# First weights in column pieces over two queues, and masked copies and taps at other steps, in a gated-merge decoder layer

## The chip, the cores and the metric

The kernel runs on one core of a Trainium2 chip (trn2). The metric is device time in microseconds (us): the median over runs of the whole program. A difference of a few tenths of a per cent is what such a comparison of this kernel can tell.

## The reference

One layer of a decoder works on 256 tokens of 2048 features. All weights are f32.

```python
h = rmsnorm(x, norm_mix_g)
c, b, xa, za, q, f, iv, og, ga, gb = split(h @ w_in)   # 8 x 1024 and 2 x 2048 columns
ya = b * causal_dwconv3(c * xa, conv_w) * silu(za)     # branch A, a convolution with three taps
lb = clip(...)                                         # lower bound, from lb_param
log_f = logaddexp(log(lb), log1p(-lb) + log_sigmoid(f))
kk = (1 - lb) * sigmoid(-f)
o = hgrn2_chunked(silu(q), kk, iv, log_f)              # branch B: gated linear recurrence, 8 heads of 128
yb = per_head_rmsnorm(o) * hg_norm_g * silu(og)
m = sigmoid(ga) * (ya @ w_a_out) + sigmoid(gb) * (yb @ w_b_out)
x = x + m @ w_o
x = x + sigmoid(rmsnorm(x, ple_norm_g) @ w_ple_gate) * (p @ w_ple_proj)
return rmsnorm(x, final_norm_g)
```

Here p is a second input of 256 tokens by 256 features. The recurrence over the tokens of a head is o_t = q_t . state, with state = exp(log_f) * state + k v.

## The kernel before

**Products.** Every large product runs over a stream of weight chunks. A chunk has 256 rows (two k-tiles of 128) by 512 columns, that is 128 partitions by 1024 f32, 512 KB. TensorE multiplies in an f32 form of reduced width (fp32r), so both operands are split into a high and a low part: `split(pos)` copies a chunk with ScalarE to `whi` (L124) and subtracts with VectorE to `wlo` (L125); `put` and `put_p` do the same for the activations. Three products (high x high, high x low, low x high) for two token tiles and two k-tiles make 12 matmuls of 512 columns for each chunk (`product`, L945).

**Order.** A list of groups, and in it of chunks, is the stream: four groups for p @ w_ple_proj with one chunk each (tile name `pT`, stored in the buffers `yaTh` and `yaTl`), then w_in, w_a, w_b, w_o and w_ple_gate. The main loop goes over the positions of the stream. Ahead of the matmuls of a position it splits the chunks up to `LEAD` = 3 positions further, and behind them it advances the open epilogues by one step each. Epilogues are generators: a `yield` ends a step, so the place of a piece of work among the matmuls is set by the number of `yield`s ahead of it. A scheduler then orders each engine's instructions, and each engine runs its own in order. The high and low parts of chunks have four buffers each.

**The start.** SyncE issues nearly all DMAs, in order. The first are p (both k-tiles in one transfer, L154), the second half of chunk 0 and chunk 1 (L111), the parameters `prm_t` (L158), then chunk 2, a quarter of x, chunk 3, and so on alternately (L815 to L817). ScalarE's queue issues the first half of chunk 0 (L111). Ten matmuls on a zeroed tile warm up TensorE (`WARM`, L820 to L825). For the first chunk `put_p(i)` and a split of half i are taken in turn, and the first k-tile's products are taken by kind, high x high first, low parts of the weights last:

```python
for n in ((0,), (2,), (1,)) if pos == 0 and i == 0 else ((0, 1, 2),):
    for t in range(NT):
        product(psum[t], state[opname], k, t, hi[:, s], lo[:, s], k == 0, k == 2 * nch - 1, n)
```

**The recurrence.** `hgrn(j)`, j = 0 and 1, handles four heads each. It works on 128 tokens with a hierarchy of levels (`LEVELS`): for each level a pair of operands `X` is made, multiplied on TensorE in many small matmuls (`products`, L389), and the parts that belong to the level are kept by masked copies (`keep`, COPY_PREDICATED). The four small levels are collected in a tile `both`; two masked copies then bring `both` into the two blocks of `a` (L511). `kT` and `qT` are scaled in place (L509, L510) for the last pairs, which TensorE multiplies at L530.

**The taps.** `ep_xa(j)` multiplies c and xa, transposes the product through DRAM (`turned`) and applies the three taps of the convolution for four feature tiles: one on ScalarE (L608) and two on VectorE (L617), in steps.

Of the kernel before, what the change touches and what calls it, by code (L numbers as in the profile page):

```python
# [9 lines left out]
F32 = mybir.dt.float32  # L10
# [5 lines left out]
P = 128  # L16
T = 256
NT = T // P
# [5 lines left out]
CW = 512  # L24
PLE = 256
EPS = 1e-6
WARM = 10
LB_FLOOR = 1e-30
LB_MAX = 1.0 - 1e-6
SCAN = 64  # L30
# [14 lines left out]
def hybrid_kernel(ctx, tc, xT, x, pT, prm, gfin, masks, w_in, w_a, w_b, w_o, w_pg, w_pp, out):  # L45
    nc = tc.nc
# [31 lines left out]
    def t4(tag="t4", bufs=None):  # L78
        bufs = bufs or {"tmp1": 8, "tmp2": 5, "tmp3": 5}[state["tmp"]]
        return pools[state["tmp"]].tile([P, 1024], F32, tag=tag, bufs=bufs, name=nm(tag))  # L80
# [13 lines left out]
    def load(pos):  # L94
        w, g, c = stream[pos]
        if pos // 2 not in loaded:
            raw = wp.tile([P, 2, 2 * CW], F32, tag="raw", bufs=3, name=nm("raw"))
            loaded[pos // 2] = raw
            if FIRST <= pos < FIRST + 4:
                for i in range(2):  # L100
                    nc.sync.dma_start(out=raw[:, i, :], in_=w[g, :, c + i, :])
            elif pos >= FIRST:
                nc.sync.dma_start(out=raw, in_=w[g, :, c : c + 2, :])
        return loaded[pos // 2]

    def load_first(pos, queues):

        w, g, c = stream[pos]
        n = 2 * CW // len(queues)
        for i, eng in enumerate(queues):  # L110
            eng.dma_start(out=load(pos)[:, pos % 2, i * n : (i + 1) * n], in_=w[g, :, c, i * n : (i + 1) * n])  # L111

    def split(pos, halves=(0, 1)):
        w, g, c = stream[pos]
        src = load(pos)[:, pos % 2, :]

        pool, n = (pools["late"], 6) if (pos - state.get("late", len(steps))) % 10 < 6 and "late" in state else (wp, 4)
        if pos not in parts:
            parts[pos] = tuple(
                pool.tile([P, 2 * CW], F32R, tag=tag, bufs=n, name=nm(tag)) for tag in ("whi", "wlo")  # L120
            )
        hi, lo = parts[pos]
        s = slice(halves[0] * CW, (halves[-1] + 1) * CW)
        a = nc.scalar.activation(out=hi[:, s], in_=src[:, s], func=AF.Copy)  # L124
        v = nc.vector.tensor_tensor(  # L125
            out=lo[:, s], in0=src[:, s], in1=hi[:, s].bitcast(F32), op=ALU.subtract
        )
        state["splits"] = (a.ins, v.ins)
# [22 lines left out]
    FIRST = 6  # L151

    praw = t4()[:, : 2 * T]
    nc.sync.dma_start(out=praw.rearrange("p (k t) -> p k t", k=2), in_=pT)  # L154
    load_first(0, (nc.scalar, nc.sync))
    load_first(1, (nc.sync,))
    prm_t = const.tile([P, PRM_N], F32, name="prm_t")
    nc.sync.dma_start(out=prm_t, in_=prm)  # L158

    if PAD_CONST:  # L160
        nc.gpsimd.memset(const.tile([P, PAD_CONST], F32, name="pad"), 0.0)
# [189 lines left out]
    def hgrn(j):  # L351
# [122 lines left out]
        for i in range(4):  # L474
            keep(both, 2 + i, heads(bk), 32 * i)
        Xs.append(level(LEVELS[1]))
        yield
        yield
        yield

        e = t4()
# [25 lines left out]
        for blk in range(2):  # L507
            kk, qq = k2[:, :, blk, :, 1 - blk, 0], q2[:, :, blk, :, 1 - blk, 0]
            nc.vector.tensor_tensor(out=kk, in0=kk, in1=rv[:, :, blk], op=ALU.mult)  # L509
            nc.gpsimd.tensor_tensor(out=qq, in0=qq, in1=fv[:, :, blk], op=ALU.mult)  # L510
            nc.vector.copy_predicated(  # L511
                out=a[:, blk],
                mask=mask_t[:, len(LEVELS) + blk : len(LEVELS) + blk + 1, :].to_broadcast([P, 4, P]), data=both,
            )
        yield
        yield
        bo = bank("s")
# [75 lines left out]
    def ep_xa(j, psum):  # L593
        cx = t4()
        plain_times(psum, state["c", j], cx)
        cxT = yield from turned(cx, 4)
        cv = t4("cv", 1)
        for h in range(2):
            for i in range(2):
                n = h * 2 + i  # L600
                k = j * 4 + n
                d, s = cv[:, n * T : (n + 1) * T], cxT[:, n * T : (n + 1) * T]

                def w(tap):
                    c = PRM_CONV + tap * 8 + k
                    return prm_t[:, c : c + 1]

                nc.scalar.activation(out=d, in_=s, func=AF.Identity, scale=w(2))  # L608

                for tap, to, fr, n_ in (  # L610
                    (1, 1, 0, P - 1), (1, P, P + 1, P - 1), (1, T - 1, P - 1, 1),
                    (0, 2, 0, P - 2), (0, P, P + 2, P - 2), (0, T - 2, P - 1, 1), (0, T - 1, P - 2, 1),
                ):
                    if (tap, to) == (0, 2):
                        yield
                        yield
                    nc.vector.scalar_tensor_tensor(  # L617
                        out=d[:, to : to + n_], in0=s[:, fr : fr + n_], scalar=w(tap), in1=d[:, to : to + n_],
                        op0=ALU.mult, op1=ALU.add,
                    )  # L620
                if n < 3:
                    yield
                    yield
        state["cv", j] = cv

    def ep_za(j, psum):
# [186 lines left out]
        )  # L813

    for c in range(4):  # L815
        load_first(c + 2, (nc.sync,))
        load_x(c)  # L817


    warm = pools["tmp1"].tile([P, 4, P], F32, tag="both", bufs=1, name="warm")  # L820
    nc.vector.memset(warm[:, :2, :], 0.0)
    warm = warm[:, :2, :].rearrange("p h t -> p (h t)").bitcast(mybir.dt.bfloat16)
    wb = bank("s")
    for _ in range(WARM):
        nc.tensor.matmul(wb, warm[:, :P], warm, start=True, stop=True)  # L825

    def put_x(k):
        put(state["hT"], k, xraw[k // 4][:, (k % 4) * T : (k % 4 + 1) * T], gain(PRM_GMIX, k))
# [119 lines left out]
    for pos, (gi, c) in enumerate(steps[:last_group]):  # L948
        kind, j, w, g, opname = groups[gi]
        nch = w.shape[2]  # L950
        if kind == "PG" and j == 0 and c == 0:
            close_pool("m")
            open_pool("late", "left")
            state["late"] = done
        order = ExitStack()
        if 1 <= pos <= 4:

            order.enter_context(tc.issue_after(state["evicted"]))
        while done < min(pos + 1 + ahead(pos), len(steps)):
            if done == 0:  # L960
                for i in range(2):
                    put_p(i)
                    split(done, (i,))
            else:
                for k in range(2 * (done - 4), min(2 * (done - 4) + 2, KT)) if done >= 4 else ():
                    put_x(k)
                split(done)
            done += 1
        order.close()
        if 2 <= pos < 6:  # L970
            load_x(pos + 2)
        if pos == 4:
            begin()
        if 0 <= pos - NORM < 4:
            add_squares(pos - NORM)
        if pos == NORM + 3:
            norm_of_x()
        if pos == NORM + 4:
            active.append(ep_f(0, waiting))
            step(active[-1])  # L980
            nc.sync.dma_start(out=mask_t, in_=masks)
        if c == 0:
            psum = [bank("s" if kind == "PP" and j > 1 else "g") for _ in range(NT)]
        hi, lo = parts.pop(pos)
        for i in range(2):
            k = 2 * c + i
            s = slice(i * CW, (i + 1) * CW)
            for n in ((0,), (2,), (1,)) if pos == 0 and i == 0 else ((0, 1, 2),):
                for t in range(NT):
                    product(psum[t], state[opname], k, t, hi[:, s], lo[:, s], k == 0, k == 2 * nch - 1, n)  # L990


        if kind == "PG" and j == 0 and c < 2:
            advance()
        for q in range(done, min(done + AHEAD, len(steps)) if pos >= FIRST else 0):
            load(q)
        if 0 <= pos - TOKENS < 4:
            load_tokens(pos - TOKENS)
        if kind != "PG" or j or c >= 2:
            advance()  # L1000
        if kind == "O" and j == 0 and c == nch - 3:
            finish()
            third_part()
        if kind == "O" and j > 0 and c == 1:
            residual(j)
        if kind == "O" and j == 2 and c == 4:
            load_gfin()
        if kind == "PG" and c == 4:
            load_projection(j)
            if j == 2:  # L1010
                load_projection(3)
        if c == nch - 1:
            if kind == "f" and j == 0:

                waiting = psum
            if kind == "ga" and j == 0:
                finish()
                second_part()
            if kind == "O" and j == 0:
                state["x1T"] = operand(big, "x", KT)  # L1020
            if kind == "f" and j == 0:
                continue
            active.append(epilogues[kind](j, psum))
            step(active[-1])
# [99 lines left out]
```

## Time and profile before

| | us |
|---|---|
| median of 3 runs | 826.5 (826.21 to 826.66) |
| profiled execution | 827.48 |
| its span | 825.0 |
| around the span | 2.48 |

The page belongs to the profiled execution; its times count from the start of the span. The mean granted TensorE clock is 0.996. PE is TensorE's matmuls and PEld its weight loads, DVE is VectorE, ACT ScalarE, POOL GpSimd, SP SyncE; a name with q behind it (SPq) is the engine's sequencer, which issues DMAs. In the timeline a row gives start, duration, engine, line, operation, tiles and shapes, how many instructions were merged, and in brackets the idle time before it and what ended it. L12 is line 12 of the kernel.

### The profile page before, as it was taken

To read this page: it belongs to the slowest core of one execution; us is meant where nothing else is said; L and a number is where in the kernel's file an instruction comes from. 1 tells how busy PE (TensorE), PEld (TensorE's weight loads), DVE (VectorE), ACT (ScalarE), POOL (GpSimd) and SP (SyncE) were. 2 spreads that over 40 slices of the span, in tenths; PEclk is the share of its full clock that TensorE was granted. 3 is DMA by queue.
4 is the path that set the end of the run, shared out by engine and by line. 5 is a ranking of instruction groups with operands and counts; after the bars stand their busy time and mean duration, and the time that the engine had idled before them with its cause. 6 is when DMAs were issued, how large, how long until landed. Compare 5 with 4: busy or idle time off the path is not lost.

```text
span 825.0 us, 10664 instructions
## 1 busy us (share of the span) xinstructions
PE 814.1 (99%) x4186; PEld 674.1 (82%) x4186; DVE 533.1 (65%) x616; ACT 431.6 (52%) x555; POOL 86.8 (11%) x74
## 2 busy tenths in 40 slices
PE   9999999999999999999999999999999999999995
PEld 6888888888888888888888888888888888888885
DVE  5747698966766598977645546545544656679633
ACT  7667465455564465466443543544444455566522
POOL 1000045200000064100001001000100000001210
PEclk9999999999999999999999999999999999999998
DMA  9969656648776664748555755756755787887702
GB/s 340 371 262 339 219 189 207 209 154 263 245 235 226 205 205 160 249 155 286 200 185 186 264 187 174 253 202 204 245 182 192 248 293 274 303 301 269 292 1 103
DMA packets 40659, 187.25 MB, mean 227 GB/s; under 512 B 4640, under 2 KB 13856, under 8 KB 22432
## 3 DMA queue, kind: packets, MB, share of 16 engines
q1 hardware_dynamic: 40176, 185.78, 65.8%
q10 hardware_dynamic: 432, 0.79, 0.3%
q8 instruction: 32, 0.52, 0.2%
q14 instruction: 19, 0.16, 0.1%
HBM read 172.92 MB, written 13.63 MB: 226 GB/s over the span
## 4 chain that ended last, share of the span: by engine, by line
PE 96%; issue 1%; DMA 1%; DVE 0%; ACT 0%; SPq 0%; POOLq 0%; POOL 0%
PE g L945 94%; PE s L945 1%; PE s L389 1%; DMA raw<-in_w_pp 1%; PE s L520 0%; PE s L544 0%; PE s L543 0%; PE s L542 0%; ACT xs L778 0%; DVE wlo L125 0%; ACT whi L124 0%; DVE t L748 0%; DVE t L752 0%; DVE xs L751 0%; POOLq L1119 0%
## 5 line engine op out<-in xcount | busy, mean ns | idle before, releaser
L125 DVE TENSOR_TENSOR wlo<-raw,whi 128x1024 fp32r<-128x1024 f32 (+1 forms) x293 | 365.5, 1253 | 252.3 <-ACT whi L124 251.5
L124 ACT ACTIVATE whi<-raw 128x1024 fp32r<-128x1024 f32 (+1 forms) x293 | 307.6, 1056 | 334.4 <-PE g L945 291.9
L945 PE MATMUL g<-whi,xh 128*128 128x512 f32 (+1 forms) x912 | 351.8, 387 | 0.5 <-issue 0.5
L945 PE MATMUL g<-wlo,xh 128*128 128x512 f32 (+1 forms) x912 | 351.9, 386 | 0.0
L945 PE MATMUL g<-whi,xl 128*128 128x512 f32 (+1 forms) x912 | 351.8, 386 | 0.0
L945 PEld LDWEIGHTS g<-whi,xh 128*128 128x128 f32 x912 | 171.4, 188 | 35.0 <-issue 1.0
L945 PEld LDWEIGHTS g<-whi,xl 128*128 128x128 f32 x912 | 171.4, 188 | 34.4
L945 PEld LDWEIGHTS g<-wlo,xh 128*128 128x128 f32 x912 | 171.5, 188 | 34.0
L945 PE MATMUL g<-whi,mh 128*128 128x512 f32 x128 | 49.8, 390 | 0.0
L945 PE MATMUL g<-wlo,mh 128*128 128x512 f32 x128 | 49.7, 390 | 0.0
L945 PE MATMUL g<-whi,ml 128*128 128x512 f32 x128 | 49.6, 390 | 0.0
L672 POOL TENSOR_TENSOR t<-ga,gb 128x512 f32<-128x512 f32 x6 | 10.6, 1788 | 198.1 <-DVE gb L667 198.1
L945 PEld LDWEIGHTS g<-whi,mh 128*128 128x128 f32 x128 | 24.0, 188 | 5.2 <-ACT mh L678 0.3
L945 PEld LDWEIGHTS g<-whi,ml 128*128 128x128 f32 x128 | 24.0, 188 | 5.1 <-DVE ml L679 0.2
L945 PE MATMUL g<-whi,yaTh 128*128 128x512 f32 x72 | 28.1, 395 | 0.0
L945 PE MATMUL g<-wlo,yaTh 128*128 128x512 f32 x72 | 28.0, 391 | 0.1
L945 PEld LDWEIGHTS g<-wlo,mh 128*128 128x128 f32 x128 | 24.0, 188 | 4.9
L945 PE MATMUL g<-whi,yaTl 128*128 128x512 f32 x72 | 27.9, 390 | 0.0
L443 POOL TENSOR_TENSOR t<-b 128x512 f32<-128x512 f32 x10 | 20.4, 2036 | 68.2 <-DVE b L319 41.1
L945 PE MATMUL g<-whi,ybTl 128*128 128x512 f32 x64 | 24.9, 389 | 0.0
L945 PE MATMUL g<-whi,ybTh 128*128 128x512 f32 x64 | 24.9, 389 | 0.0
L945 PE MATMUL g<-wlo,ybTh 128*128 128x512 f32 x64 | 24.9, 389 | 0.0
(156 smaller groups left out, 515.3 us busy)
## 6 DMA issues: line engine op xcount, KB each, us to landing
raw<-in_w_in SPq DMA_DIRECT2D x93, 1024.0 KB, 5.0
raw<-in_w_o SPq DMA_DIRECT2D x16, 1024.0 KB, 5.3
raw<-in_w_pg SPq DMA_DIRECT2D x16, 1024.0 KB, 5.8
turn<-t SPq DMA_DIRECT2D x72, 128.0 KB, 2.6
t<-turn SPq DMA_DIRECT2D x18, 512.0 KB, 5.1
raw<-in_w_a SPq DMA_DIRECT2D x8, 1024.0 KB, 5.2
raw<-in_w_b SPq DMA_DIRECT2D x8, 1024.0 KB, 5.1
raw<-in_w_in SPq DMA_DIRECT2D x6, 512.0 KB, 7.8
```

The costliest lines, as they stand in the source:

```text
L124: a = nc.scalar.activation(out=hi[:, s], in_=src[:, s], func=AF.Copy)
L125: v = nc.vector.tensor_tensor(out=lo[:, s], in0=src[:, s], in1=hi[:, s].bitcast(F32), op=ALU.subtract)
L389: nc.tensor.matmul(heads(bk)[r, h, c if at is None else slice(at, at + 32)], key(h)[:, r], query(h)[:, c], start=True, stop=True, tile_pos ...
L443: nc.gpsimd.tensor_tensor(out=er, in0=br, in1=ref, op=ALU.subtract)
L672: (nc.vector if j == 3 else nc.gpsimd).tensor_tensor(out=spread(m, t), in0=blocks(ga[:, s]), in1=blocks(gb[:, s]), op=ALU.add)
L945: nc.tensor.matmul(psum, a, b, start=first and n == 0, stop=last and n == 2)
```

## The change

- p comes in two transfers, one for each k-tile, both on SyncE's queue.
- The first half of chunk 0 comes in two pieces of 256 columns, both on ScalarE's queue; its second half stays on SyncE's queue. Chunk 1 comes in halves, the first on ScalarE's queue, the second on SyncE's, behind p's second k-tile.
- The parameters are loaded behind chunk 2.
- Chunk 0 is split, and its first k-tile multiplied, in pieces of 256 columns; chunk 1 is split in halves (`EARLY`).
- The warm-up has 7 matmuls, on a constant of ones that is there before the program begins; the memset goes.
- In `hgrn` the two copies of `both` into `a` move ahead, into steps that were empty.
- In `ep_xa` two steps are put in ahead of the taps and two are dropped between them.

```diff
-WARM = 10
+WARM = 7
+
+EARLY = {0: ((0, CW // 2), (CW // 2, CW), (CW, 2 * CW)), 1: ((0, CW), (CW, 2 * CW))}
...
-    def split(pos, halves=(0, 1)):
+    def split(pos, c0=0, c1=2 * CW):
...
-        s = slice(halves[0] * CW, (halves[-1] + 1) * CW)
+        s = slice(c0, c1)
...
-    nc.sync.dma_start(out=praw.rearrange("p (k t) -> p k t", k=2), in_=pT)
-    load_first(0, (nc.scalar, nc.sync))
-    load_first(1, (nc.sync,))
+    def load_p(k):
+        nc.sync.dma_start(out=praw[:, k * T : (k + 1) * T], in_=pT[:, k, :])
+
+    def load_columns(pos, c0, c1, eng):
+        w, g, c = stream[pos]
+        eng.dma_start(out=load(pos)[:, pos % 2, c0:c1], in_=w[g, :, c, c0:c1])
+
+    load_p(0)
+    load_columns(0, 0, CW // 2, nc.scalar)
+    load_columns(0, CW // 2, CW, nc.scalar)
+    load_columns(1, 0, CW, nc.scalar)
+    load_columns(0, CW, 2 * CW, nc.sync)
+    load_p(1)
+    load_columns(1, CW, 2 * CW, nc.sync)
     prm_t = const.tile([P, PRM_N], F32, name="prm_t")
-    nc.sync.dma_start(out=prm_t, in_=prm)
...
         Xs.append(level(LEVELS[1]))
-        yield
-        yield
+        for blk in range(2):
+            yield
+            keep(a[:, blk], len(LEVELS) + blk, both)
         yield
...
             nc.gpsimd.tensor_tensor(out=qq, in0=qq, in1=fv[:, :, blk], op=ALU.mult)
-            nc.vector.copy_predicated(
-                out=a[:, blk],
-                mask=mask_t[:, len(LEVELS) + blk : len(LEVELS) + blk + 1, :].to_broadcast([P, 4, P]), data=both,
-            )
...
         cxT = yield from turned(cx, 4)
+        yield
+        yield
         cv = t4("cv", 1)
...
                 if n < 3:
                     yield
-                    yield
+                    if n < 1:
+                        yield
...
     for c in range(4):
-        load_first(c + 2, (nc.sync,))
+        load_columns(c + 2, 0, 2 * CW, nc.sync)
+        if c == 0:
+            nc.sync.dma_start(out=prm_t, in_=prm)
         load_x(c)
...
-    warm = pools["tmp1"].tile([P, 4, P], F32, tag="both", bufs=1, name="warm")
-    nc.vector.memset(warm[:, :2, :], 0.0)
-    warm = warm[:, :2, :].rearrange("p h t -> p (h t)").bitcast(mybir.dt.bfloat16)
+    ones = [nc.const_aps.tensor(1.0, [P, n], mybir.dt.bfloat16) for n in (P, CW)]
     wb = bank("s")
     for _ in range(WARM):
-        nc.tensor.matmul(wb, warm[:, :P], warm, start=True, stop=True)
+        nc.tensor.matmul(wb, *ones, start=True, stop=True)
...
-            if done == 0:
-                for i in range(2):
-                    put_p(i)
-                    split(done, (i,))
-            else:
+            for c0, c1 in EARLY.get(done, ((0, 2 * CW),)):
+                if done == 0 and c0 % CW == 0:
+                    put_p(c0 // CW)
                 for k in range(2 * (done - 4), min(2 * (done - 4) + 2, KT)) if done >= 4 else ():
                     put_x(k)
-                split(done)
+                split(done, c0, c1)
...
-            s = slice(i * CW, (i + 1) * CW)
-            for n in ((0,), (2,), (1,)) if pos == 0 and i == 0 else ((0, 1, 2),):
-                for t in range(NT):
-                    product(psum[t], state[opname], k, t, hi[:, s], lo[:, s], k == 0, k == 2 * nch - 1, n)
+            for c0, c1 in EARLY[0][:2] if pos == 0 and i == 0 else ((0, CW),):
+                s = slice(i * CW + c0, i * CW + c1)
+                for n in ((0,), (2,), (1,)) if pos == 0 and i == 0 else ((0, 1, 2),):
+                    for t in range(NT):
+                        product(
+                            psum[t][:, c0:c1], state[opname], k, t, hi[:, s], lo[:, s], k == 0 and c0 == 0, k == 2 * nch - 1, n
+                        )
```

More of the change, by code (lines that the diff above doesn't have):

```diff
@@ L104, in load @@
         return loaded[pos // 2]
[L106 to L111, printed above, removed]
-    def split(pos, halves=(0, 1)):
+    def split(pos, c0=0, c1=2 * CW):
         w, g, c = stream[pos]
```

## The prediction, made before the changed kernel was run

> **What bounds the kernel now.** I read the page's parts 1 and 4 first, then the chain in order of time, then the timeline of the first 12 us, and last the windows.
>
> ```profile
> span 825.0 us, 10664 instructions
> PE 814.1 (99%) x4186; PEld 674.1 (82%) x4186; DVE 533.1 (65%) x616; ACT 431.6 (52%) x555; POOL 86.8 (11%) x74
> ```
>
> TensorE is busy for 99% of the span, VectorE for 65%. A microsecond is gained only where TensorE stands still or starts late, and whatever it loses is not given back. The chain says where it stood still (start, duration, what):
>
> ```profile
> 1.65 5.16 DMA raw<-in_w_pp
> 6.83 1.07 ACT whi L124
> 7.93 1.24 DVE wlo L125
> 9.21 2.56 PE g L945 x10
> ...
> 17.21 119.68 PE g L945 x528
> ...
> 165.26 1.60 PE g L945 x6
> 166.87 0.54 issue
> 167.41 9.84 PE g L945 x42
> ```
>
> One 512-column matmul costs 119.68 / 528 = 0.2267 us. The last place where data held TensorE is 9.21 us: the low half `wlo` of chunk 1 (the second chunk of weights), behind its load and its high half `whi`. From there TensorE runs through to the end, but for 0.54 us at 166.87 that no data explains. So this change is decided in the first 12 us, with those 0.54 us as a side issue. The timeline of the start:
>
> ```profile
> 0.74 0.39 SPq L154 DMA_DIRECT2D t<-in_pT  x1
> 0.74 0.40 ACTq L111 DMA_DIRECT2D raw<-in_w_pp  x1
> 1.19 4.45 PE L825 MATMUL s<-warm 128*128 128x512 bf16 x10 [1.19 <-DVE warm L821]
> 2.44 0.15 PEld L825 LDWEIGHTS <-warm 128*128 128x128 bf16 x1 [0.28 <-issue]
> 2.87 0.15 PEld L825 LDWEIGHTS <-warm 128*128 128x128 bf16 x1 [0.28 <-issue]
> 4.48 0.49 DVE L897 CAST yaTh<-t 128x256 fp32r<-128x256 f32 x2 [3.35 <-DMA t<-in_pT]
> 4.68 1.17 ACT L124 ACTIVATE whi<-raw 128x512 fp32r<-128x512 f32 x2 [2.01 <-DMA raw<-in_w_pp]
> 4.89 0.42 DVE L898 TENSOR_TENSOR yaTl<-t,yaTh 128x256 fp32r<-128x256 f32 x1
> 5.34 0.69 DVE L125 TENSOR_TENSOR wlo<-raw,whi 128x512 fp32r<-128x512 f32 x1
> 5.36 1.02 PE L945 MATMUL g<-whi,yaTh 128*128 128x512 f32 x2
> 6.21 0.63 PE L945 MATMUL g<-whi,yaTl 128*128 128x512 f32 x2
> 8.44 1.06 ACT L124 ACTIVATE whi<-raw 128x1024 fp32r<-128x1024 f32 x1 [0.54 <-DMA raw<-in_w_pp]
> 9.53 1.23 DVE L125 TENSOR_TENSOR wlo<-raw,whi 128x1024 fp32r<-128x1024 f32 x1 [0.38 <-ACT whi L124]
> 11.61 0.39 PE L945 MATMUL s<-whi,yaTh 128*128 128x512 f32 x1
> ```
>
> The first real matmul starts at 5.36, behind the first `whi`; chunk 2 starts at 11.61. That 11.61 is my yardstick: the change gains or loses what chunk 2 starts earlier or later. Its floor is the row at 9.53: `wlo` of chunk 2 is ready at 10.76 and the chunk's second matmul needs it, so no more than about 0.8 us can be gained while chunk 2's load comes when it comes now.
>
> **The loads.** What the DMA engines moved (columns: stretch, its length, busy time of PE, PEld, DVE, ACT, POOL, granted clock, DMA share, GB/s):
>
> ```profile
> 0.00:2.00 2.00, 0.81 (x2) 0.28 (x3) 0.27 (x1) 0.83 (x1) 1.47 (x9) 1.00 0.14 28
> 2.00:3.00 1.00, 1.00 (x4) 0.43 (x3) 0.00 (x0) 0.66 (x2) 0.82 (x3) 1.00 0.52 166
> 3.00:4.00 1.00, 1.00 (x4) 0.32 (x3) 0.00 (x0) 0.00 (x0) 0.00 (x0) 1.00 1.01 367
> 4.00:5.00 1.00, 1.00 (x3) 0.30 (x2) 0.52 (x3) 0.32 (x1) 0.00 (x0) 1.00 1.09 399
> 5.00:6.00 1.00, 1.00 (x4) 0.55 (x3) 0.97 (x3) 0.85 (x2) 0.30 (x1) 1.00 1.09 365
> 6.00:7.00 1.00, 1.00 (x6) 0.82 (x5) 0.97 (x3) 0.17 (x1) 0.22 (x1) 1.00 0.93 311
> ```
>
> Summed, 222 KB had moved by 3.0 us, 589 by 4.0, 988 by 5.0, 1353 by 6.0. From 3 us on the engines are full (share about 1), so only the order of the bytes counts. p and the first half of chunk 0 (524 KB, one on each queue) are complete at 3.82 by this sum and used at 4.48 and 4.68; p, chunk 0 and chunk 1 (1311 KB) at 5.88, used at 6.83. A load is used 0.65 to 0.95 us after its bytes have gone by; I take 0.85. SP's and ACT's queue got about equal shares.
>
> In the changed kernel, SP's queue holds p's k-tile 0 (131 KB), the second half of chunk 0 (262), p's k-tile 1 (131), half of chunk 1; ACT's holds the first quarter of chunk 0 (131), its second quarter (131), the other half of chunk 1 (262). With equal shares:
> - k-tile 0 and the first quarter: 262 KB, 3.1 us, used at 3.95.
> - k-tile 1: 524 KB of its own queue and as many of the other's, 1049 KB, 5.17, used at 6.0. Bounds: 5.35 if ACT's half of chunk 1 takes nothing before it (786 KB, 4.49), 6.3 if it is as late as chunk 1 was.
> - all of p, chunk 0 and chunk 1: the same 1311 KB, used at 6.8 as now. The parameters go behind chunk 2; being 37 KB, they give chunk 2 0.1 us.
>
> **What that makes of the start.** The order in which VectorE's instructions stand is: cast of k-tile 0, its low part, then **the cast of k-tile 1**, and only then `wlo` of the first quarter, `wlo` of the second, k-tile 1's low part, `wlo` of the second half, both halves of chunk 1. VectorE works in order, so the two first `wlo` stand behind a load that they do not need, and TensorE, in order too, stands at its third pair of matmuls. (Now p comes in one load, and nothing waits like this.) Step by step:
> - `whi` of the first quarter: 3.95 plus about 0.35 (half of 1.17 / 2, with an overhead), TensorE begins at 4.4, an estimate, 1.0 us earlier than now.
> - It does four matmuls of 256 columns and stops for `wlo` by 5.3.
> - VectorE: k-tile 1 at 6.0, cast 0.25 (half of 0.49), `wlo` of 256 columns 0.42 (the 128x256 row at 4.89): 6.67, TensorE at 6.72.
> - Left of chunks 0 and 1 are 24 - 2 = 22 matmuls' worth: 22 x 0.2267 = 4.99, plus 0.13 for the restart (from 9.21 to 11.61 ten matmuls took 2.40 and not 2.27). Chunk 2 starts at 11.84: **0.23 us later than now**. With the bounds of k-tile 1: 0.42 earlier to 0.53 later.
> - Hidden behind it: VectorE's other five pieces take 0.42 + 0.42 + 3 x 0.69 = 2.91 and are through by 9.6, each ahead of its matmul; chunk 2's `wlo` then follows its `whi` at 9.5 as now. ACT issues two more DMAs (2 x 0.40 us) before it loads its table, and has until 3.95.
> - The splitting adds six matmuls, but of half size, so nothing in columns. The warm-up loses three matmuls and the wait for VectorE's memset (1.19); it ends near 3.9 (0.9 + 3.0) instead of 5.6, and is covered by the loads.
>
> **The masked copies and taps.** VectorE and TensorE at that place:
>
> ```profile
> 159.34 1.16 DVE L125 TENSOR_TENSOR wlo<-raw,whi 128x1024 fp32r<-128x1024 f32 x1
> 160.74 0.75 DVE L511 COPY_PREDICATED a<-mask_t,both 128x512 f32<-128x512 int32 x1
> 161.40 0.40 DVE L509 TENSOR_TENSOR kT<-kT,t 128x256 f32<-128x256 f32 x1
> 164.48 0.67 PEld L389 LDWEIGHTS s<-qT,kT 128*32 128x32 f32 x64
> ```
>
> Both copies of `both` into `a` move ahead of the reciprocals, to steps where the scheduler put them around a `wlo`. VectorE is dense there, so `kT`'s second product ends one copy later, 161.8 + 0.7 = 162.5; TensorE wants it at 164.48: hidden, 2 us to spare. The `wlo` in between come up to 1.4 us later, and they are made three chunks ahead of their use (LEAD is 3: 3 x 12 x 0.2267 = 8.2 us): hidden. The taps begin two steps later and drop two steps between them, so they end in the same step, and no operation is added. Without the cover a copy costs 0.75. I count zero for both `hgrn` calls, with 0 to 0.75 as bounds. SP's queue, where a `turn` could move, sees no changed order after the start.
>
> **The gap at 166.87.** No row names a releaser. What the page does show is TensorE's code:
>
> ```profile
> q8 instruction: 32, 0.52, 0.2%
> ```
>
> That is 32 pieces of 16 KB for 2 x 4186 instructions, about 262 each. The gap comes six matmuls after a burst of 160 small ones, so I take it as code that came late. The change shifts everything behind the start by +12 (six matmuls with their weight loads) - 6 (warm-up) + 1 (a wait) = 7 instructions: the piece's edge is reached 3.5 matmuls, up to 0.8 us, earlier, while the order for it goes out earlier by that much too if it goes out before the burst, and by almost nothing inside it. So 0 to 0.7 longer; I take 0.2, being nearest to the row of 0.54 as it stands. If another shift happens to free it, 0.54 are gained.
>
> **Sum.** 0.23 + 0 + 0.2 = 0.4 us later. The profiled execution took 827.48 (span 825.0, 2.48 around it), 0.98 above the median of 826.5; I carry the difference over: 827.9 for a profiled execution, **826.9** for the median.
>
> **Rivals.**
> (1) *The clock, slower.* The warm-up's weight loads stand 0.43 us apart (2.44, 2.87) against 0.23 for a matmul later: TensorE began at half speed, and by the rows at 5.36 (two in 1.02) and 6.21 (two in 0.63) it changed near 6, some 5 us after the first matmul at 1.19. It also falls back when idle:
>
> ```profile
> 815.00:816.00 1.00, 0.95 (x8) 0.75 (x7) 0.00 (x0) 0.01 (x1) 0.00 (x0) 1.00 0.00 0
> 816.00:817.00 1.00, 0.00 (x0) 0.00 (x0) 0.47 (x2) 0.47 (x1) 0.00 (x0) 1.00 0.00 0
> 818.00:819.00 1.00, 0.00 (x0) 0.00 (x0) 0.33 (x2) 0.29 (x1) 0.55 (x1) 0.69 0.00 0
> ```
>
> The last matmuls end near 816; the mean of 0.69 puts the halving of the clock at 818.4, 2.4 us later. In the changed kernel TensorE works from about 0.9 to 3.9 (seven matmuls, 7 x 0.43 = 3.0 us), rests half a microsecond, works 0.9, and stands from 5.3 to 6.7. If these pauses keep it from speeding up, it restarts at 6.72 at half speed for 3 to 5 us, and half of that, 1.5 to 2.5, is lost: **829.0**. It decides from the point at which the pauses (1.9 of the 5.8 us up to 6.7) are enough for the clock to stay down; for it speaks that three warm-up matmuls are gone, against it that the real ones begin earlier and that a pause of 1.4 is shorter than 2.4. The Trainium skill, "TensorE: Matmul & The Clock Gate" (Part 1, What's actually happening), says that full speed is granted after one busy window of about 3.4 us and that the windows run freely. By that rule 3.0 us of warm-up fill no window, ten (4.3 us) do, and this rival would come true when the gaps count as not busy. The rows agree as far as they go (5 us here); what share of a window counts as busy no row shows.
> (2) *Earlier, a gain.* k-tile 1 lands at its early bound and the gap at 166.87 closes: -0.42 - 0.54, **825.6**; with one of the two, 826.0. For it: loads in smaller pieces can pass each other. Against: the engines are full from 3 us on.
> (3) *VectorE's cover fails* at the copies, 0.75 in each `hgrn`: with the forecast's 0.4, **828.3**. Against: 2 us to spare.
>
> **Chances.** Forecast 0.50 (826.4 to 827.5), clock 0.23 (828.1 to 829.6), gain 0.22 (825.4 to 826.4), cover 0.05. About 0.2% of 826.5, 1.65 us, is what a measurement of this kernel can tell from no change: 824.85 and 828.15. Slower by more: most of the clock's cases and half of the cover's, 0.21. Faster by more: the floor of 0.8 and the gap's 0.54 together stay inside it, 0.03. Range 825.7 to 829.0: left out are some 0.07 of the gain and 0.1 of the clock.
>
> **What would show it.** Right: VectorE idle until about 6.0 ahead of the second cast; TensorE's first real matmul near 4.4, a wait for `wlo` until 6.7, chunk 2 at 11.8. Wrong: a second cast before 5.4, or matmuls still 0.43 apart after 6.7, or a new wait for `kT` or `a`.

## The result, and the profile after

| | before | after |
|---|---|---|
| median, us | 826.48 (826.21 to 826.71) | 829.98 (828.07 to 831.58) |
| profiled execution, us | 827.48 | 828.07 |
| its span, us | 825.0 | 826.2 |

The ratio is 1.0043 (95% interval 1.0032 to 1.0053): 3.5 us slower, outside the range of the prediction, and on the side to which it gave 0.21. The profiled execution of after is the shortest of its six, so the trace shows the kernel at its best. That it comes near the 827.9 forecast for a profiled execution is luck: its span is 1.2 longer than before's, but the time around the span is 1.87 instead of 2.48. The head of its page, the span and the busy times:

```profile
span 826.2 us, 10676 instructions
PE 813.3 (98%) x4189; PEld 674.1 (82%) x4189; DVE 530.5 (64%) x617; ACT 431.8 (52%) x557; POOL 87.7 (11%) x74
```

TensorE has three matmuls more and as much to do as before; again a loss must be time in which it stands still or runs slowly. The chain of after in order of time (start, duration, what):

```profile
1.65 4.77 DMA t<-in_pT
...
6.66 0.43 DVE wlo L120
7.13 5.32 PE g L951 x26
...
17.89 119.68 PE g L951 x528
...
165.94 0.67 PE g L951 x2
166.61 1.19 issue
167.80 10.61 PE g L951 x46
```

The chain now begins with p, and not with the weights. It joins TensorE at 7.13, and the stretch of 528 matmuls starts at 17.89 instead of 17.21. The gap behind the burst of small matmuls is 1.19 us instead of 0.54. The timeline of the start of after:

```profile
0.78 3.15 PE L831 MATMUL s<-const-bfloat16-1.0 128*128 128x512 bf16 x7 [0.78 <-PEq L1121]
4.04 0.80 PE L951 MATMUL g<-whi,yaTh 128*128 128x256 f32 x2
4.63 0.63 PE L951 MATMUL g<-whi,yaTl 128*128 128x256 f32 x2
6.45 0.29 DVE L903 CAST yaTh<-t 128x256 fp32r<-128x256 f32 x1 [2.32 <-DMA t<-in_pT]
6.66 0.75 DVE L120 TENSOR_TENSOR wlo<-raw,whi 128x256 fp32r<-128x256 f32 x2
7.13 0.51 PE L951 MATMUL g<-wlo,yaTh 128*128 128x256 f32 x2 [1.87 <-DVE wlo L120]
9.29 1.06 ACT L119 ACTIVATE whi<-raw 128x1024 fp32r<-128x1024 f32 x1 [0.46 <-DMA raw<-in_w_pp]
12.29 0.39 PE L951 MATMUL s<-whi,yaTh 128*128 128x512 f32 x1
161.06 0.74 DVE L516 TENSOR_TENSOR kT<-kT,t 128x256 f32<-128x256 f32 x2
165.15 0.67 PEld L395 LDWEIGHTS s<-qT,kT 128*32 128x32 f32 x64
```

This is the picture that the prediction drew: VectorE stands at the cast of p's second k-tile, both `wlo` of the quarters stand behind it, and TensorE stands at `wlo` for 1.87 us. Chunk 2 starts at 12.29, 0.68 later than before. `kT` is ready at 161.8, and its reader begins at 165.15. The windows of after (stretch, length, busy time of PE, PEld, DVE, ACT, POOL, granted clock, DMA share, GB/s):

```profile
4.00:5.00 1.00, 0.96 (x4) 0.93 (x4) 0.13 (x1) 0.38 (x2) 0.00 (x0) 1.00 0.87 288
5.00:6.00 1.00, 0.26 (x2) 0.00 (x0) 0.00 (x0) 0.56 (x2) 0.00 (x0) 1.00 1.06 313
6.00:7.00 1.00, 0.00 (x0) 0.00 (x0) 0.55 (x3) 0.00 (x0) 0.00 (x0) 1.00 0.95 329
7.00:8.00 1.00, 0.87 (x7) 0.88 (x8) 1.00 (x4) 0.32 (x1) 0.00 (x0) 1.00 0.93 283
5.40:8.80 3.40, 1.67 (x11) 1.58 (x12) 2.35 (x6) 1.28 (x3) 0.00 (x0) 1.00 0.99 323
```

TensorE is idle for nearly two of four microseconds, and from 4 to 8 us the engines of the DMA move 283 to 329 GB/s where they moved 311 to 399 before. In this execution the clock held all the same.

So the trace shows 0.68 + 0.65 = 1.33 us, and the median is 3.5 above. The other executions hint at what is missing: their spans and mean clocks are 828.3 (0.995), 827.9 (0.995), 829.8 (0.992), 829.3 (0.996) and 828.1 (0.995), against 826.2 (0.997) in the profiled one. A mean clock lower by 0.002 over 826 us is 1.65 us of TensorE's time. But the mean is a coarse measure. It counts the end of the span, where TensorE is done and the clock falls (at 818.4 in before, at 821.2 in after), and it counts as full speed whatever comes ahead of the first change, the slow warm-up too. Executions of before range from 0.995 to 0.998. So these figures suggest that the clock's rival was at work in executions that no trace had caught yet, and do not show it. One more profile of the same kernel was taken for that reason.

> The changed kernel itself, for a second trace: its profiled execution so far, 828.07, is the fastest of its six. If the clock is what spreads its times: in an execution of 829.8 or more the clock is taken back for about 3.4 us in the pause (up near 4 us, half near 7.5, up near 11), chunk 2 starts at 13.5 to 14.5 us instead of 12.3 us, or the clock comes up only near 9 to 10 us. If something else spreads them: chunk 2 at 12.3 us again and a loss elsewhere.

It took 831.71 us, span 829.9, mean clock 0.992. TensorE's and VectorE's rows in its timeline:

```profile
4.43 0.40 PE L951 MATMUL g<-whi,yaTl 128*128 128x256 f32 x2
7.20 0.29 DVE L903 CAST yaTh<-t 128x256 fp32r<-128x256 f32 x1 [3.05 <-DMA t<-in_pT]
7.88 0.80 PE L951 MATMUL g<-wlo,yaTh 128*128 128x256 f32 x2 [3.05 <-DVE wlo L120]
10.61 0.63 PE L951 MATMUL g<-wlo,yaTh 128*128 128x512 f32 x1
11.04 0.63 PE L951 MATMUL g<-whi,yaTl 128*128 128x512 f32 x1
15.80 0.39 PE L951 MATMUL s<-whi,yaTh 128*128 128x512 f32 x1
```

```profile
3.70:7.00 3.30, 0.89 (x5) 0.54 (x4) 0.43 (x1) 1.27 (x3) 0.00 (x0) 1.00 0.94 292
7.10:13.80 6.70, 5.92 (x18) 5.05 (x19) 5.55 (x9) 4.58 (x8) 0.00 (x0) 0.50 1.04 393
13.90:16.00 2.10, 2.10 (x10) 1.72 (x10) 1.64 (x3) 1.91 (x3) 0.00 (x0) 1.00 1.06 408
```

The first fence is the timeline, the second the windows. p's second k-tile came 0.75 later than in the other execution, the pause was 3.05, and from 7.1 to 13.8 the granted clock is 0.50: the matmuls at 10.61 and 11.04 stand 0.43 apart instead of 0.23. Ahead of the pause the clock was up already: the pair at 4.43 takes 0.40, and 0.63 at 4.63 in the profile above, where it came up later. Chunk 2 starts at 15.80, 3.5 later than in the profile above.

### The profile page after: what moved, and what is told of

It reads as the page before. It is cut to its first block, busy times and chain, and to the rows that moved or that the text cites. A ratio compares the mean times of both kernels' runs of the same rounds, so it can differ in the third digit from the quotient of the medians.

```text
span 826.2 us, 10676 instructions
## 1 busy us (share of the span) xinstructions
PE 813.3 (98%) x4189; PEld 674.1 (82%) x4189; DVE 530.5 (64%) x617; ACT 431.8 (52%) x557; POOL 87.7 (11%) x74
## 3 DMA queue, kind: packets, MB, share of 16 engines
q10 hardware_dynamic: 720, 1.05, 0.3%
## 4 chain that ended last, share of the span: by engine, by line
PE 97%; issue 1%; DMA 1%; DVE 0%; ACT 0%; SPq 0%; POOLq 0%; POOL 0%; DVEq 0%
PE g L951 94%; PE s L951 1%; PE s L395 1%; DMA t<-in_pT 1%; PE s L523 0%; PE s L546 0%; PE s L547 0%; PE s L545 0%; ACT xs L784 0%; DVE t L754 0%; DVE t L758 0%; DVE xs L757 0%; POOLq L1127 0%; POOL r L779 0%; ACT t L753 0%
## 5 line engine op out<-in xcount | busy, mean ns | idle before, releaser
L951 PE MATMUL g<-wlo,yaTh 128*128 128x512 f32 (+1 forms) x74 | 28.1, 385 | 1.9 <-DVE wlo L120 1.9
L951 PE MATMUL g<-whi,yaTh 128*128 128x512 f32 (+1 forms) x74 | 28.3, 389 | 0.1
L951 PE MATMUL g<-whi,yaTl 128*128 128x512 f32 (+1 forms) x74 | 28.3, 387 | 0.0
```

The lines of the kernel that those rows point to most:

```text
L951: nc.tensor.matmul(psum, a, b, start=first and n == 0, stop=last and n == 2)
```

## The experiments

The theory after the result: VectorE's cast stands ahead of work that is ready, TensorE's pause follows, and in most executions the clock falls over that pause; the gap at 166 us adds its part. The rivals: the masked copies and taps, the shorter warm-up, the slower loads. Times are medians with their range, compared with before in the same comparison (826.56 to 826.70 throughout).

**Which half of the change.** `e1_middle_only` is before with the copies and taps moved; `e2_start_only` is after with both put back.

```diff
# e1_middle_only, on before (and the four lines of the copies at their old place go)
-        yield
-        yield
+        for blk in range(2):
+            yield
+            keep(a[:, blk], len(LEVELS) + blk, both)
...
+        yield
+        yield
...
-                    yield
+                    if n < 1:
+                        yield
```

> The kernel before with the masked copies and the taps at the new steps alone. If the moved steps cost nothing (the prediction's step): 826.5, within 0.3. If they carry the loss: 828 to 830, with a TensorE wait for kT, a or wlo in the trace near 163 us or 345 us. The gap near 166.9 us stays at 0.5 us, since TensorE's code is the same.

> The changed kernel with copies and taps at the old steps. If the start carries the loss: about 830, spread over some 3 us as in the changed kernel. If the moved steps carry it: 826.5 to 827.

e1 took 826.97 (826.56 to 828.09), ratio 1.0003 [0.9994, 1.0012]; e2 830.16 (827.66 to 830.91), ratio 1.0036 [1.0023, 1.0048]. e2's trace shows a wait for `wlo` of 3.08 and the half clock from 7.44 to 10.85. The copies and taps cost nothing that can be measured; the start carries the loss.

**The order of VectorE's queue.** `e3_cast_behind` is after with the cast of k-tile 1 and its low part behind `wlo` of both quarters.

```diff
-                if done == 0 and c0 % CW == 0:
-                    put_p(c0 // CW)
+                if done == 0 and c0 == 0:
+                    put_p(0)
+                if done == 0 and c0 == CW:
+                    with tc.issue_after(state["splits"][1]):
+                        put_p(1)
```

> The changed kernel, with the cast and the low part of p's second k-tile queued on VectorE behind wlo of the two 256-column pieces; the loads are the same. If the pause of 1.9 us behind that cast is what costs (directly and through the clock): no wait for wlo at 5.2 us, chunk 2 starts at 11.4 to 11.6 instead of 12.3 us, and the median falls to 827 to 827.5 with a spread under 1 us. If the seven warm-up matmuls are too few whatever follows: the median stays at 829 or more and the spread at 3 us.

827.66 (827.25 to 829.9), ratio 1.0017 [1.0008, 1.0026]: 2.3 us of the 3.5 come back. In its trace the matmuls are at full speed from 6.47 on and chunk 2 starts at 11.69. A gap of 0.9 near 166 us stays. The spread is a miss, 2.7 us and not under 1: two of the eleven executions took 829.75 and 829.9, with a mean clock of 0.994. So the start can still go wrong with the cast behind; why is open, no trace shows such an execution.

**The warm-up's length.** `e4_warm10` is after with ten warm-up matmuls.

```diff
-WARM = 7
+WARM = 10
```

> The changed kernel with ten warm-up matmuls instead of seven, the pause behind the cast left as it is. They end near 5.1 us, 1.1 us after the first whi. If the shorter warm-up is what costs: 827.5 to 828, with a spread under 1 us. If the pause is: 829.5 or more. Chunk 2 starts at 12.3 us either way, since wlo comes at 7.1 us. TensorE's code is 6 instructions longer than the changed kernel's, so the gap near 166.6 us may differ from 1.2 us.

830.31 (828.83 to 830.97), ratio 1.0039 [1.0026, 1.0051]: as slow as after. In its trace the clock went up at 4.44, by the spacing of the matmuls, and fell again at 7.86, over a wait for `wlo` of 2.36. The missing warm-up matmuls were not the cause; it is the pause behind them.

**p in one transfer.** `e5_p_whole` keeps all of after but p's two transfers.

```diff
-    load_p(0)
+    nc.sync.dma_start(out=praw.rearrange("p (k t) -> p k t", k=2), in_=pT)
...
-    load_p(1)
```

> The changed kernel with p in one transfer again, in the place of its first k-tile; all else as changed. If the late second k-tile is the cause: both casts run at about 4.0 us, no pause for wlo, chunk 2 at 11.4 to 11.7 us, median 827.5 to 827.8 (what is left over before is the longer gap near 166 us). If the column pieces and the second queue themselves cost: 829 or more.

827.97 (826.37 to 828.33), ratio 1.0011 [1.0002, 1.0020]. TensorE's rows in its timeline:

```profile
4.96 0.79 PE L950 MATMUL g<-whi,yaTh 128*128 128x256 f32 x2 [1.04 <-ACT whi L119]
8.15 0.63 PE L950 MATMUL g<-wlo,yaTh 128*128 128x512 f32 x1
8.58 0.53 PE L950 MATMUL g<-whi,yaTl 128*128 128x512 f32 x1
9.18 0.39 PE L950 MATMUL g<-wlo,yaTh 128*128 128x512 f32 x1
```

No wait for `wlo` is left, but the matmuls are 0.43 apart until about 8.8: the warm-up ended a microsecond before the first real matmul, and the clock had not come up. Chunk 2 starts at 12.35, later than the 11.4 to 11.7 expected, and the casts run at 4.29 and not at 4.0. The median is 2.0 below after, so the split of p carries the larger part of the loss.

**The gap near 166 us.** If it is TensorE's code that comes late, it must depend on how many instructions stand ahead of it, and on nothing else. `e6_before_warm7` takes three warm-up matmuls (six instructions) out of before; `e7_before_code8` and `e13_before_code20` put four and ten tiny ones in.

```diff
# e6_before_warm7
-WARM = 10
+WARM = 7
# e7_before_code8, range(10) in e13_before_code20
+    for _ in range(4):
+        nc.tensor.matmul(wb[:, :4], warm[:, :P], warm[:, :4], start=True, stop=True)
```

> The kernel before with seven warm-up matmuls instead of ten. They end near 4.2 us, the first whi comes at 5.3 us. If the clock needs the warm-up as such: 827.5 to 828.5. If a pause of 1 us that the real matmuls follow closely does not matter: 826.4 to 827.0. TensorE's code is 6 instructions shorter, so the gap near 166.9 us may shrink by up to 0.6 us.

> The kernel before with four more warm-up matmuls of 4 columns: 8 instructions more in TensorE's code, some 0.1 to 0.3 us of work ahead of the first loads, all hidden. If the gap near 167 us is code that comes late, and shifting the code makes it longer: the gap grows from 0.7 to 1.2 or 1.5 us (start to start, above the usual spacing) and the time by 0.5 to 0.8, to 827.2 to 827.5. If the gap has another cause: 826.7, the gap as it was.

> The kernel before with ten warm-up matmuls of 4 columns more: 20 instructions. The run with the idle matmuls alone had 19 more than the kernel before. If the gap near 167 us grows on with the shift, to 2 to 3 us: 828.0 to 829.0, and that hides what the idle matmuls gained. If it stays as with 8 instructions more: 827.5, and the miss of that run has another cause.

e6 took 827.13 (825.65 to 828.18), 1.0003 [0.9994, 1.0012], with spans of 823.9 to 824.0 in four executions and of 825.0 to 825.7 in seven; e7 827.52 (827.03 to 828.02), 1.0011 [1.0002, 1.0019]; e13 828.26 (827.7 to 829.27), 1.0020 [1.0010, 1.0029]. The chains near 166 us, of e6, of e7 and of e13:

```profile
163.79 1.34 PE s L389 x109
165.13 11.11 PE g L945 x48
```

```profile
163.73 1.34 PE s L389 x109
165.07 0.66 PE g L947 x2
165.73 1.76 issue
```

```profile
163.80 1.31 PE s L389 x106
165.11 1.84 issue
```

Nothing differs between these kernels but the warm-up, 160 us earlier. With six instructions fewer the gap is gone from the trace, with eight or twenty more it is 1.8 us. It also moves: in before it comes six large matmuls behind the burst, in e7 two behind it, and in e13 four small matmuls ahead of the burst's end. A matmul and its weight load are two instructions, so eight instructions moved it by four matmuls and twelve more by six. A gap that moves back by the number of instructions is a place in the code. e13's time lies in the range expected for a gap that grows on, but the gap did not grow: it is 1.84 and in e7 1.76. Of the 0.7 us between the two medians the traces show 0.2 (chunk 2 at 11.50 and 11.42, and the gap). e6's profiled execution has a span of 823.9 without the gap; why seven of its eleven executions take 1.1 to 1.8 more is open, no trace was taken of one.

**Both repairs.** `e8_cast_code59` is e3 with 33 warm-ups of 108 columns instead of 7 of 512, as long in time, and 59 instructions more than before.

```diff
-WARM = 7
+WARM = 33
-    ones = [nc.const_aps.tensor(1.0, [P, n], mybir.dt.bfloat16) for n in (P, CW)]
+    ones = [nc.const_aps.tensor(1.0, [P, n], mybir.dt.bfloat16) for n in (P, 108)]
-        nc.tensor.matmul(wb, *ones, start=True, stop=True)
+        nc.tensor.matmul(wb[:, :108], *ones, start=True, stop=True)
```

> The changed kernel with the second cast queued behind wlo, as in the run before of that name, and the warm-up as 33 matmuls of 108 columns instead of 7 of 512: the same 3 us, but 52 instructions more, 59 more than the kernel before. If TensorE's code comes in pieces of 256 instructions and the gap arises where a piece begins just behind the burst near 166 us, this puts the edge inside the burst, ordered ahead of it: no gap over 0.2 us there or near 348 us, and 826.3 to 826.8. If the gap is tied to the burst and not to an edge: it stays at 0.7 to 1.4 us, and 827.5.

825.79 (825.24 to 826.36), ratio 0.9991 [0.9982, 1.0000]: 1.9 below e3, 4.2 below after, 0.9 below before, and faster than expected. Its chain near 166 us, and its timeline at the start:

```profile
163.38 1.34 PE s L395 x109
164.72 11.11 PE g L951 x48
```

```profile
4.08 0.42 DVE L120 TENSOR_TENSOR wlo<-raw,whi 128x256 fp32r<-128x256 f32 x1
6.00 0.29 DVE L903 CAST yaTh<-t 128x256 fp32r<-128x256 f32 x1
11.07 0.39 PE L951 MATMUL s<-whi,yaTh 128*128 128x512 f32 x1
```

The gap is gone, `wlo` of the first quarter is made at 4.08 while k-tile 1 is still under way, and chunk 2 starts 0.54 earlier than before. It is the fastest kernel here, though at the edge of what the comparison can tell from before.

**The clock by itself.** `e9_fill_pause` is after with six idle matmuls of 512 columns in the pause, ahead of the first use of `wlo`: TensorE stays busy, VectorE's queue stays as it is.

```diff
+                    if pos == 0 and i == 0 and c0 == 0 and n == (1,):
+                        for _ in range(6):
+                            tc.keep_in_program_order(nc.tensor.matmul(wb, *ones, start=True, stop=True))
```

> The changed kernel with six idle matmuls of 512 columns on the constant, put where TensorE pauses for the first wlo; the second cast still stands ahead of wlo, so nothing of the real work comes earlier. If the pause costs through the clock: the clock is never taken back in the trace, chunk 2 stays near 12.3 to 13 us, and the median falls from 830 to 827.8 to 828.8, with a spread under 2 us. If the loss is only the waiting itself: 830, as the changed kernel.

A miss: 830.49 (828.51 to 831.55), ratio 1.0038 [1.0026, 1.0049]. In its trace (828.72) the clock stayed up from 5.84 on, by the spacing of the matmuls, but the twelve instructions of the filling made the gap 1.8 us, which e13 repeats without them. And two executions near 828.6 have a mean clock of 0.997, the four above 830 one of 0.995 or 0.996, which suggests that the filling did not hold the clock each time; no trace was taken of those four. So the same was tried where the code is out of the way. `e10_after_code59` is after with the 33 short warm-ups of e8 and nothing else; `e12_fill_code71` is e10 with the six idle matmuls.

> The changed kernel with the warm-up as 33 matmuls of 108 columns, 59 instructions more than the kernel before, and the cast left where it is. If code and pause add: no gap near 166 us, 1.2 to 1.6 us less than the changed kernel, 828.4 to 828.9, with the spread of 3 us left. If the gain of the run with both came from the cast alone: 830.

> The changed kernel with 33 short warm-up matmuls (as the run of that kind before, 828.3) and the six idle matmuls in the pause, the cast left ahead of wlo: 71 instructions more than the kernel before, so no gap near 166 us. The run with the idle matmuls alone did not get faster; in its trace the clock stayed up, but the gap was 1.76 us. If the clock taken back in the pause is what is left of the loss: 826.5 to 827.3, the clock up by 6 us and never taken back, chunk 2 at 12.3 to 12.8 us. If it is not: 828.3 again.

e10 took 828.31 (827.44 to 829.81), 1.0018 [1.0010, 1.0027]; e12 827.17 (826.63 to 827.98), 1.0007 [0.9998, 1.0016]. Neither trace has the gap. The windows of e10, then of e12:

```profile
4.00:7.30 3.30, 0.74 (x4) 0.54 (x4) 0.60 (x4) 0.94 (x2) 0.00 (x0) 1.00 0.97 292
7.40:10.70 3.30, 3.29 (x12) 3.00 (x13) 2.95 (x6) 2.21 (x3) 0.00 (x0) 0.50 1.04 400
```

```profile
4.00:7.40 3.40, 3.24 (x10) 1.66 (x10) 0.33 (x3) 0.94 (x2) 0.00 (x0) 1.00 0.88 295
7.40:10.80 3.40, 3.02 (x17) 2.59 (x18) 3.24 (x7) 2.21 (x3) 0.00 (x0) 1.00 1.04 404
```

With TensorE busy for 0.74 of 3.3 us the next 3.4 run at half speed; filled up to 3.24 of 3.4 they run at full speed. By the medians, idle matmuls that compute nothing are worth 1.1 us. Chunk 2 starts at 13.05 in e12, a little later than expected.

**An earlier k-tile 1.** `e11_p_first` is e8 with p's second k-tile ahead of the second half of chunk 0 on SyncE's queue.

```diff
     load_columns(1, 0, CW, nc.scalar)
-    load_columns(0, CW, 2 * CW, nc.sync)
     load_p(1)
+    load_columns(0, CW, 2 * CW, nc.sync)
     load_columns(1, CW, 2 * CW, nc.sync)
```

> The run with the cast behind wlo and 33 warm-up matmuls, with p's second k-tile loaded ahead of the second half of chunk 0. If p's second k-tile is still what the second k-tile's products wait for: its cast before 5.5 us, and 825.3 to 825.8. If the second half of chunk 0 becomes what they wait for: no difference, 825.8, or 0.2 more.

A miss: 828.07 (825.84 to 829.43), ratio 1.0010 [1.0000, 1.0020]. In its timeline the cast comes at 5.03, but the weights pay for it:

```profile
5.03 0.28 DVE L903 CAST yaTh<-t 128x256 fp32r<-128x256 f32 x1
8.44 0.50 PE L951 MATMUL g<-whi,yaTh 128*128 128x512 f32 x1 [1.58 <-ACT whi L119]
10.56 0.63 PE L951 MATMUL g<-whi,yaTl 128*128 128x512 f32 x1
```

```profile
6.58:9.99 3.41, 1.60 (x6) 0.89 (x6) 1.57 (x4) 1.83 (x4) 0.00 (x0) 1.00 1.02 389
```

TensorE waits 1.58 us for `whi` of chunk 0's second half instead, from 6.86 to 8.44. It works again from there, and yet the granted clock falls to a half at 9.99 and comes back at 13.40. The second fence is the stretch of 3.41 us ahead of that fall: TensorE was busy for 1.60 us of it. So a pause shorter than the 1.87 of the profile of after was enough here. With the engines of the DMA busy (a share of 0.91 from 4 to 8 us), an earlier transfer makes another one late.

## Why the prediction was wrong

The way from after (829.98) down to e8 (825.79) by medians, taken in two ways:

| step | one way | the other |
|---|---|---|
| gap of the code | after to e10: 1.7 | e3 to e8: 1.9 |
| clock over the pause | e10 to e12: 1.1 | after to e3, both together: 2.3 |
| the pause itself | e12 to e8: 1.4 | |
| sum, after to e8 | 4.2 | 4.2 |

Of these 4.2 us 3.5 are after's loss, and the rest is e8's gain on before (0.9, with 0.2 between the medians of before in the two comparisons). Before has a gap of about 0.5 us of its own, so not all of the first line is new in after. The lines are not clean either: e8's loads came sooner than those of the others, and chunk 2 starts at 11.07 in its trace, at 11.69 in e3's and at 13.05 in e12's. So 0.6 of the 1.9 lies at the start, and the 1.4 of the pause holds the faster loads as well.

- **VectorE's order and the pause: right.** The cast stands ahead of both `wlo`, TensorE starts at 4.04 (4.4 forecast) and stops for `wlo`; e3 shows it by turning the order round.
- **k-tile 1 at 6.0: mis-sized.** It came at 6.45 and 7.20 in the two profiles of after, and between 6.60 and 7.15 in e2, e3, e4, e9, e10 and e12. The forecast's own upper bound, 6.3, was passed each time, and it does not follow from its reason ("as late as chunk 1 was"): chunk 1 was used at 6.83. The step that failed is the sum behind 6.0, by which the k-tile is used 0.85 us after 1049 KB have gone by. The lower rate (303 GB/s from 4 to 8 us, 365 in before) is the smaller part of it. Summed over the windows, 953 KB had gone by at 5.0 in the profile of after and 917 in e14, and 1049 at 5.31 and 5.49, against 5.17 forecast; but the k-tile was used 1.14 and 1.71 us later than that. And e8, with 933 KB at 5.0, has the k-tile at 6.00. Whether bytes of other loads went ahead of it or its own took longer to land stays open. So the pause was 1.87 and 3.05 us instead of 1.4. Chunk 2's load, forecast 0.1 earlier, was used 0.85 later (`whi` at 9.29 and 8.44).
- **The clock: nearly the right mechanism, put at nothing in the sum and given too small a chance.** Rival (1) has the clock stay down behind the pauses; in e14, e2, e4 and e10 it was up and was taken back. The price, 1.5 to 2.5, fits: one window of 3.4 us at half speed costs 1.7. The rival got 0.23 because a pause of 1.4 is shorter than the 2.4 us after which the clock fell at the end of before. This argument failed too. In e14 TensorE stops at 4.83 and the clock falls at 7.07, in e10 at 4.74 and 7.37, so 2.2 and 2.6 later, as in before. But in e11 a pause of 1.58 was followed by the fall, 3.1 us after its start, when TensorE had long been at work again. What fits these traces is that the work in a whole window counts, and so also where the windows lie: e14 had its clock up ahead of the pause and lost it, the profile of after got it only near 5.26 or later and kept it. Of the five traces with the cast ahead and nothing in the pause (after, e2, e4, e10, e14) four show the fall. Whether it would have come less often with the forecast's pause of 1.4, no run shows. After's execution of 831.04 with a mean clock of 0.996 stays unexplained; a clock that came up late, as in e5's trace with a mean of 0.997, would not show in that figure.
- **The gap: right in kind, mis-sized.** "0 to 0.7 longer; I take 0.2": it is 0.65 longer in the profile of after, 0.9 in e14, and the shift of 7 lies just where the step from no gap (-6) over 0.5 (0) to 1.8 (+8) is steepest. To take the value nearest to the row as it stands was no reason on such a slope.
- **Copies and taps at zero: right** (e1), with 3.4 us to spare between `kT` at 161.8 and 165.15, where 2 was forecast.
- **The warm-up: right that it is covered**, and its length isn't what the clock turned on (e4), though with p whole (e5) the clock did come up late behind it.

## What to carry to other kernels

When a load is split so that its first part is used early, look at what the second part's consumer stands ahead of on its engine: here one cast that waited for its bytes held up ready work and turned a gain into a pause. Price a pause of TensorE near the start by the whole window in which it falls, not by its own length. And where a short burst of small matmuls is followed by an "issue" gap, shift the code by some dozens of instructions before looking for a data dependence.

## What the runs showed of the hardware

**The clock is granted by windows.** In the traces of e2, e4, e10 and e11 the half clock lasts 3.41 us, in e14 6.8, twice as long, though TensorE was busy for 5.92 of 6.7 us there. The 3.41 us ahead of a fall held 0.71 us of matmuls in e2, 0.74 in e10, 0.93 in e14, 1.05 in e4 and 1.60 in e11. A stretch with 1.67 of 3.4 us (after, 5.40 to 8.80) kept full speed, but as nothing falls there, the trace doesn't show where its windows lie. So a window that was 47% busy was too little once; a threshold isn't shown. The Trainium skill, "TensorE: Matmul & The Clock Gate" (Part 1, What's actually happening), states a free-running window of about 3.4 us and only two speeds, and the traces agree with both, 3.41 and 0.50. It gives the fall as following an idle window; here windows that were 21% to 47% busy were enough.

**Late code.** Pieces of 16 KB hold about 262 instructions by the prediction's count. That they are TensorE's fits their number: 32 in before, e1 and e6, and 33 in all kernels with seven or more instructions added. I take the gap for the next piece, which a burst of 160 small matmuls in 2.4 us asks for sooner than it comes; that it hangs on the place in the code is shown, that it is the fetch is argued. The gap by the number of instructions that a kernel has ahead of the burst more than before:

| instructions | -6 | 0 | 7 | 8 | 13 | 19, 20 | 59, 71 |
|---|---|---|---|---|---|---|---|
| gap, us | 0 (e6) | 0.4 to 0.5 (e1, before) | 0.9 to 1.5 (after, e2, e3, e5, e14) | 1.8 (e7) | 1.5 (e4) | 1.8 (e9, e13) | 0 (e8, e10, e11, e12) |

The Trainium skill, "Runtime: NRT & Kernel Launch" (Instruction fetch mechanics), says that code comes in blocks of 16 KiB, one ahead, and that this is hidden behind the pace of issue; the blocks agree, but in this burst up to 1.8 us are not hidden.

**A slower burst of loads.** From 4 to 8 us the DMA moved 365 to 411 GB/s in the kernels with p in one transfer (before, e1, e5, e6, e7, e13) and 299 to 336 with p by k-tiles (after, e2, e3, e4, e9, e10, e11, e12, e14), but 367 in e8, which splits p as well. What makes it so is not settled: e8 differs from e10 in the place of one cast, and no run varied the transfers alone further than e5.
